# A diffusion step on one core: a third of four weight folds in the opening stage, projection inputs two tiles ahead, attention products two units behind the scores, queries one unit earlier

## The chip, the cores and the metric

The kernel runs on one core of a Trainium2 chip. The metric is the device time of one execution in microseconds (us). The times before are 1214.49, 1209.16 and 1210.06, median 1210.06 us. A profile is one execution recorded by the hardware profiler; the engines in it are PE (TensorE), DVE (VectorE), ACT (ScalarE), POOL (GpSimd) and SP (SyncE, which here only issues transfers).

## The reference

The reference is one inference step of a small hybrid backbone: 256 context tokens and 1024 latent tokens, width 1024, two layers, all in f32.

Layer 0 norms and modulates the tokens (a shift, scale and gate from SiLU(c) through a weight matrix), multiplies them by one combined input projection and splits the result into two mixers, each with 8 query heads, 2 key/value heads of 64, and a SiLU gate path. Mixer A is global attention with norms on queries and keys and rotary positions. Mixer B is attention in a window of ±128 tokens, with a learned sink logit for each head. Context tokens read only context; latent tokens read their latent keys (all, or those of the window), the context keys of this step and 256 cached context keys. The gated outputs of both mixers go through one output projection and are added to the tokens.

Layer 1 replaces attention by a Fourier mixer, and a final norm follows:

```
h  = modulate(rms_norm(x))
u  = h @ w_u                       # 1024 -> 4 groups of 256 channels
z  = Re(FFT2(u))                   # over positions and channels of a group
x += gate * ((z * silu(h @ w_g)) @ w_out)
```

## The kernel before, in words

**Tiles.** The 1280 tokens are ten row tiles of 128: tiles 0 to 7 are latent, 8 and 9 context. Matrix products run on PE as three products of a high and a low half (mm3, line 263), so each input and weight is split first: a cast to the high half on ACT or DVE (L275, L277), then a subtraction for the low half on DVE or POOL (L281).

**Folds.** The Fourier transform over the channels of a group is a matrix product with fixed matrices. It is folded into the weights of layer 1 ahead of their use: for each of the four channel groups, fold_load brings two 128×1024 tiles of the transposed weight (L542, tile w), fold_piece multiplies a quarter of them with the transform's matrix (L557, tile wa, 8 matmuls a piece, four pieces a fold), and fold_put stores the result to DRAM (L547, wd), from which layer 1 reads it. Folds 0 and 1 are done in the opening, folds 2 and 3 during attention.

**The opening stage.** PH0 (L32) is a list of operations written out by hand, in which the program runs them: f, the loads of a fold; F, a piece of a fold; G, a store of two pieces; w and s, the loads of projection weights and the end of their split; x and N, the loads and norms of tokens; L, A and M, the loads, matmuls and end of the modulation (ada, L467; modt, L516; the modulation vectors, L479 and L484); T, the transposes of normed tokens (xt, L424), and X, Y, Z their modulation; K and R, parts of the first projection (kv0s, kv2s, L526); S, small loads. SP issues transfers in the order of the list; the order on the other engines is the scheduler's.

**Order elsewhere.** The framework orders the instructions of each engine with a list scheduler that runs on a timeline of its own, so a small change of the program re-orders every engine. Buffers come from zones (ZONES, L23): a zone holds a number of buffers, and an instruction that takes one waits until its last user is through. The zone q (queries) holds two, the zone p (scores and probabilities) four.

**Attention.** A unit is one row tile, one key/value head and one pair of query heads (t, g, pr); a mixer has 40. `attend` (L1077) runs over a list of units. For each it issues the score matmuls and the softmax (`soft`, L932: sL and sC, L924, and sB, L996, on PE; L958 and L1002 on DVE; the exponential, L965, on ACT), keeps the unit pending, and issues the transposes of the probabilities and the products with the values (`weigh`, L1031: pt, L1041, and av, L1047, on PE; the split of pt on ACT, L275, and DVE, L1044; the result, L1058) once more than LAG units are pending: LAG_A = 1 in mixer A, LAG_B = 3 in mixer B. The queries of a tile and head come from DRAM (load_q, tile q); `attend` loads the next ones when it is at pair QPRE of the present tile:

```python
            if pr == QPRE and nx is not None and nx not in qs and ("q", nx[0] // 2 * 2, nx[1]) in fl_.done:
                qs[nx] = load_q(*nx)
```

**Filler.** After each unit a queue of other work is pumped by a budget of microseconds (FILL_A, FILL_B, FILL_C), so that PE has matmuls while softmax runs on the other engines: gates and queries, then the late folds named in FLATE (L65), then the output projection, tile by tile. An item with a condition (`ready=`) holds up the queue until the condition is met.

**Output projection.** It runs over ten row tiles in five pairs, (0,4), (2,6), (3,7), (1,5), (8,9). proj_load (L1306, through proj_in, L1206) brings a tile's attention result, gate and softmax total (od, gd, scd) from DRAM and scales them on DVE (L1216, L1217), before the split on ACT (L275) and POOL or DVE; proj_step (L1315, through out_proj, L1230) is the projection itself (oz, L263), its results taken out by DVE (L1238, L1239). Each tile's load is queued just ahead of the step of the tile before. can_run (L1379) lets an item run within attention only for the first two pairs, and only when the attention units it reads have been through for some units; what is left is run after attention by `fl_.drain()`.

Of the kernel before, what the change touches and what calls it, by code (L numbers as in the profile page):

```python
# [22 lines left out]
ZONES = {"u": (26, 1032), "w": (8, 1032), "q": (2, 1024), "pt": (3, 1024), "p": (4, 1280), "h": (9, 512), "e": (4, 256)}  # L23
BIG = ("w", "q", "pt", "p", "u")
UV = ("u",)
FILL_A, FILL_B, LAG_A, LAG_B = 4.4, 2.9, 1, 3
E_PH, E_OH, E_OL, E_WO = "a", "a", "dp", "a"
EARLY, SPAN = 1, 2
WSTEP = ((2, 1, 2), (1, 0, 1))
ORD_B = (0, 2, 3, 4, 7, 6, 5, 1, 8, 9)  # L30
AT_K, AT_Q, AT_X, NX1, GL = 1, 2, 5, 7, 3
PH0 = """f0 S0 x0 N0 f1 L0 F00 F01 F02 F03 w0 L1 F10 F11 F12 F13 x1 A0 T0 T1 s0 M0 X0 X1 T2 L2 N1 K0 K1  # L32
 A1 T3 M1 G00 G01 G10 G11 L3 X2 X3 K2 K3 Y0 R0 Y1 R1 w1 S1 T4 A2 x2 N2 Y2 T5 M2 R2 X4 Y3 X5 R3
 K4 Y4 K5 A3 T6 Y5 M3 R4 X6 T7 R5 X7 Y6 K6 Y7 K7 R6 R7"""
S1 = """s1 S2 V Z0 Z1 c0 I0 a2 Z2 Z3 c1 I2 a1 q0 P Z4 Z5 I4 a2 P Z6 Z7 I6 a1 q2 P a2 P k8 a2 P a3 P a9 P"""
ADA_Z = (("p", "pt", "q"),) * 4
# [1 line left out]
XZ = ("u", "u", ("p", "pt", "q"))  # L38
E_ML = ("dp", "dp", "d")
E_MF, E_MH, LC0 = "da", "d", "ppd"  # L40
EF = 2
QPRE, HOLD = 1, 0
PLACE = (
    ((0, 0, 128),), ((128, 0, 128),), ((385, 0, 127), (256, 127, 1)), ((257, 0, 128),), ((769, 1, 127), (512, 0, 1)),
    ((896, 0, 128),), ((641, 0, 128),), ((513, 0, 128),), ((1024, 0, 128),), ((1153, 0, 127), (1152, 127, 1)),
# [16 lines left out]
FILL_C, NLATE = 2.9, 8  # L62
E_FQ, E_GD = "d", "d"
ORDER = "qa0 qa1 kb0 qb0 qb1 g0 g1 g2 g3"
FLATE = "f2 f3"  # L65
AT_B = "s"
AT_F = (0, 1, 2)
AT_N, AT_Z = (0, 0, 3, 0, 3, 2, 2, 2, 2, 2, 3, 3, 3), ("p", "pt", "q")
# [71 lines left out]
def hybrid_step(ctx: ExitStack, tc: tile.TileContext, I, O):  # L140
# [15 lines left out]
    def take(tag, shape, dt=F32):  # L156
        tags = (tag,) if isinstance(tag, str) else tag
        z = min((t for t in tags if spare[t]), key=lambda t: spare[t][0])
        i = spare[z].popleft()[1]
        size = 2 if dt == BF16 else 4  # L160
        for s in shape[1:]:
            size *= s
        assert size <= 4 * ZONES[z][1]
        made[0] += 1
        return Buf(z, i, up.tile(list(shape), dt, tag=f"{z}{i}", name=f"{z}{made[0]}", bufs=1))

    def drop(*bufs):
        for b in bufs:
            stamp[0] += 1
            spare[b.zone].append((stamp[0], b.idx))  # L170
# [380 lines left out]
    def fold_piece(g, kb2, wu, first=False):  # L551
        f = fold["f"]
        acc = bank("t" if first else "g", f"wa{g}{kb2}")
        for i in range(2):
            c0 = (2 * kb2 + i) * P
            for j in range(2):
                pe.matmul(  # L557
                    acc[:, i * 256 : i * 256 + 256], wu[j][:, c0 : c0 + P], f[:, j, :], start=j == 0, stop=j == 1
                )
        if first:  # L560
            if kb2 % 2 == 0:
                early[g, kb2 // 2] = take("u", (P, 4, 256))
            wo = early[g, kb2 // 2][:, 2 * (kb2 % 2) : 2 * (kb2 % 2) + 2, :]
        else:
            wb = take("h", (P, 2, 256))
            wo = wb.a
        copy("wo", "a", wo, acc.rearrange("p (i f) -> p i f", i=2))
        if not first:
            fold_put(g, kb2 * 256, wo)
            drop(wb)  # L570
        if kb2 == 3:
            drop(*wu)
            fold["n"] = fold.get("n", 0) + 1
            if fold["n"] in (EF, 4):
                drop(f)
                del fold["f"]
# [35 lines left out]
    def first_step(op):  # L612
        nm, i = op[0], int(op[1:])
        if nm == "L":
            ada[i] = ada_load(i, ADA_Z[i])
        elif nm == "S":
            small_loads(i)
        elif nm == "x":
            load_x(i, XZ[i])
        elif nm == "N":  # L620
            norm_rows(i)
        elif nm == "w":
            W[i] = load_w(w0cols((C_KA, C_QA)[i]), lc=LC0, later=w_fin.setdefault(i, []))
        elif nm == "s":
            for fin in w_fin[i]:
                fin()
        elif nm == "f":
            wu0[i] = fold_load(i, 2)
        elif nm == "F":
            fold_piece(i // 10, i % 10, wu0[i // 10], True)  # L630
        elif nm == "G":
            e = early.pop((i // 10, i % 10))
            fold_put(i // 10, i % 10 * 512, e.a)
            drop(e)
        elif nm == "A":
            ada_chunk(i, ada.pop(i))
        elif nm == "M":
            ada_fin(i)
        elif nm == "T":
            XT[0, i] = x_T(0, i)  # L640
        elif nm in "XYZ":
            g = "XYZ".index(nm)
            mod_T(g, i, E_ML[g])
        elif nm in "KR":
            t = 4 * "KR".index(nm)
            gemm_chunk(acc0[t], t, W[0], i)
            gemm_chunk(acc0[t + 2], t + 2, W[0], i)
        else:
            return False
        return True  # L650

    region = tc.manual_schedule(engines={sp.engine})
    region.__enter__()
    for op in PH0.split():
        first_step(op)
# [184 lines left out]
    fl_ = Filler()  # L840
# [343 lines left out]
    OB, late = [("u", "w")], [False]  # L1184
# [21 lines left out]
    def proj_in(src, gate, r, resid):  # L1206
        if gate is not None:
            flush_held()
            ol = take(OB[0], (P, 8, P))
            sp.dma_start(ol.a, src[r])  # L1210
            gl = take(OB[0], (P, 8, P))
            rl = take(OB[0], (P, 8, P))
            sp.dma_start(gl.a, gate[r])
            for h in range(2):
                sp.dma_start(rl[64 * h : 64 * h + 64], scd[r, h].partition_broadcast(64))
            pick("pm", XE["pm"]).tensor_mul(gl.a, gl.a, rl.a)  # L1216
            pick("pm", XE["pm"]).tensor_mul(ol.a, ol.a, gl.a)  # L1217
            drop(gl, rl)
        hi, lo = take(OB[0], (P, 8, P), F32R), take(OB[0], (P, 8, P), F32R)
        if gate is not None:  # L1220
            split(hi.a, lo.a, ol.a, E_OH, E_OL)
            drop(ol)
        else:
            for c in range(2):
                split(hi[:, 4 * c : 4 * c + 4, :], lo[:, 4 * c : 4 * c + 4, :], src(c, r), "a", "d")
        xr = take(OB[0], (P, D))
        sp.dma_start(xr.a, resid[r * P : (r + 1) * P, :])
        return hi, lo, xr
# [77 lines left out]
    def proj_load(i, j):  # L1306
        r = pairs[i][j]
        v = r // 8
        if v not in gt0:
            gt0[v] = take(OB[0], (P, D))  # L1310
            sp.dma_start(gt0[v].a, gtd[0, v].partition_broadcast(P))
        ins[r] = proj_in(od, gd, r, I["xp"])
        return 0
# [65 lines left out]
    def can_run(i, j):  # L1379
        r = pairs[i][j]  # L1380

        def fn():
            if sum(len(spare[z]) for z in OB[0]) < NSP or i > EARLY:
                return False
            return all(finished.get(t, 99) + SPAN < clock[0] for t in USES[r])
        return fn

    wgs = []
    steps = [(i, j) for i in range(5) for j in range(2)]

    def late_fold(nm):
        def fn():
            ws[nm] = fold_load(int(nm[1]))
            return 0
        return fn

    for n, nm in enumerate(FLATE.split()):
        fl_.add(0.0, late_fold(nm))
        if n == 0:
            fl_.add(0.0, lambda: proj_load(0, 0), ready=can_run(0, 0))  # L1400
        for k in range(4):
            fl_.add(FC, lambda k=k, nm=nm: fold_piece(int(nm[1]), k, ws[nm]))
    if not FLATE:
        fl_.add(0.0, lambda: proj_load(0, 0), ready=can_run(0, 0))
    for n, ij in enumerate(steps):
        if n == 8:
            fl_.add(0.0, lambda: wgs.append(load_w(I["w_g1"][:, 0:256], tags=BIG)) or 0)
        if n < 9:
            fl_.add(0.0, lambda ij=steps[n + 1]: proj_load(*ij), ready=can_run(*steps[n + 1]))
        fl_.add(7.7, lambda ij=ij: proj_step(*ij))  # L1410

    units = [(t, g, pr) for g in range(2) for t in range(NT) for pr in range(2)]
# [542 lines left out]
```

## Time and profile before

| | |
|---|---|
| times of the runs | 1214.49, 1209.16, 1210.06 us; median 1210.06 |
| the profiled execution: time, span | 1214.27 us, 1212.4 us |
| mean granted clock of PE | 0.985 |
| PE busy | 1166.8 us, 96% |
| DVE, ACT, POOL busy | 839.6, 576.6, 320.1 us |
| DMA traffic | 168.81 MB, mean 139 GB/s |
| mixer B's attention | about 540 to 815 us |

The span is the recorded part of the profiled execution; the rest of its time, 1.9 us, lies around it. A wait is the idle time of an engine ahead of an instruction, put down to the instruction or transfer that released it. The granted clock is the share of full speed at which PE was allowed to run, and a window's value is the mean over it. Sums of busy time count overlapping matmuls once; a group's duration in the timeline includes the end of its last matmul, so the pace of a stream is read from the starts.

### The profile page before, as it was taken

The page shows a single profiled execution, that of the slowest core. Times are in us where ns is not written, and L with a number is a line of the kernel's source. Part 1 is how long each engine was busy: PE and PEld are TensorE (multiplying, and loading weights), DVE is VectorE, ACT ScalarE, POOL GpSimd, SP SyncE. Part 2 cuts the span into 40 slices and gives each one's busy share as a digit, 9 for nine tenths or more (in the row PEclk, how much of TensorE's full clock was granted, in tenths as well). Part 3 has the DMA queues.
Part 4 walks back from the last instruction along what each step waited for, and adds up shares of the span by engine and source line. Part 5 has one row for each costly group of instructions (what it writes and reads, how often), then busy time and mean ns, then how long its engine had stood idle before and what let it go on. Part 6 is the DMA issues. An engine that isn't in the chain of part 4 may idle for free. (4 is left out here: it accounts for less than half of the span.)

```text
span 1212.4 us, 22083 instructions
## 1 busy us (share of the span) xinstructions
PE 1166.8 (96%) x8103; PEld 1041.6 (86%) x8103; DVE 839.6 (69%) x2000; ACT 576.6 (48%) x1159; POOL 320.1 (26%) x278
## 2 busy tenths in 40 slices
PE   7999999999999999999999999989999999999997
PEld 5787899999999998999888887868877888997886
DVE  3479788877777777678787776878756953367543
ACT  3343466555655555556566675533364224342211
POOL 2255634512332130011010114213202217245001
PEclk9899999999999999999999999989999999999999
DMA  9957412323523233344253686677214435264321
GB/s 317 360 190 260 150 59 66 103 79 108 149 64 101 60 92 113 95 120 121 74 140 81 181 256 198 181 201 219 96 44 136 152 114 169 94 200 151 121 103 53
DMA packets 129840, 168.81 MB, mean 139 GB/s; under 512 B 26298, under 2 KB 86454, under 8 KB 129732
## 3 DMA queue, kind: packets, MB, share of 16 engines
q1 hardware_dynamic: 129732, 167.40, 45.5%
q8 instruction: 64, 1.05, 0.4%
q14 instruction: 44, 0.36, 0.1%
HBM read 123.19 MB, written 44.16 MB: 138 GB/s over the span
## 5 line engine op out<-in xcount | busy, mean ns | idle before, releaser
L1044 DVE TENSOR_TENSOR pt<-pt,pt 128x512 fp32r<-128x512 f32 (+1 forms) x264 | 170.8, 658 | 50.9 <-ACT pt L275 50.1
L275 ACT ACTIVATE pt<-pt 128x512 fp32r<-128x512 f32 (+1 forms) x264 | 146.1, 575 | 83.9 <-PE pt L1041 49.0
L1047 PE MATMUL av<-pt,u 128*128 128x256 f32 x1008 | 167.3, 290 | 1.1 <-DVE e L1058 1.0
L1041 PE MATMUL pt<-identr,p 128*128 128x128 f32 x1008 | 153.7, 273 | 1.5 <-DVE pt L1044 1.5
L1047 PEld LDWEIGHTS av<-pt,u 128*128 128x128 f32 x1008 | 140.1, 190 | 6.2 <-DVE e L1058 2.0
L263 PE MATMUL q<-w,u 128*128 128x256 f32 x960 | 143.4, 287 | 0.2 <-ACT h L725 0.2
L263 PEld LDWEIGHTS q<-w,u 128*128 128x128 f32 x960 | 126.0, 189 | 5.1 <-issue 0.8
L1041 PEld LDWEIGHTS pt<-identr,p 128*128 128x128 f32 x1008 | 118.7, 141 | 7.0 <-issue 1.8
L263 PE MATMUL ga<-u,w 128*128 128x512 f32 (+1 forms) x576 | 124.2, 360 | 0.3 <-DVE h L817 0.2
L965 ACT ACTIVATE p<-p,nm 128x1280 f32<-128x1280 f32 (+1 forms) x80 | 95.3, 1192 | 53.4 <-DVE p L958 52.9
L263 PEld LDWEIGHTS ga<-u,w 128*128 128x128 f32 x576 | 93.6, 188 | 15.1 <-ACT pt L275 0.4
L281 POOL TENSOR_TENSOR w<-h,w 128x512 fp32r<-128x512 f32 x38 | 50.1, 1334 | 130.9 <-DVE w L277 100.4
L924 PE MATMUL sL<-u,q 128*128 128x512 f32 x256 | 82.4, 409 | 1.6 <-DMA q<-qd 1.6
L281 POOL TENSOR_TENSOR u<-h,u 128x512 fp32r<-128x512 f32 x24 | 33.8, 1416 | 158.7 <-ACT u L275 151.8
L965 ACT ACTIVATE p<-p,NM 128x640 f32<-128x640 f32 (+2 forms) x80 | 59.1, 739 | 24.5 <-DVE p L958 24.3
L924 PE MATMUL sC<-u,q 128*128 128x256 f32 x320 | 63.4, 297 | 4.0 <-DVE p L1002 2.0
L263 PE MATMUL oz<-u,u 128*128 128x512 f32 x208 | 60.8, 397 | 2.9 <-DVE h L1238 2.9
L263 PE MATMUL oz<-u,w 128*128 128x512 f32 x192 | 58.3, 396 | 0.0
L958 DVE TENSOR_SCALAR_CACHE_REDUCE p<-sL 128x512 f32<-128x512 f32 x64 | 43.8, 685 | 20.1 <-PE sL L924 15.3
L924 PEld LDWEIGHTS sC<-u,q 128*128 128x128 f32 x320 | 49.5, 190 | 7.7 <-DVE p L1002 2.6
L698 POOL TENSOR_TENSOR h<-h,rope 128x512 f32<-128x512 f32 (+1 forms) x18 | 21.2, 1180 | 128.2 <-ACT h L781 82.3
L958 DVE TENSOR_SCALAR_CACHE_REDUCE p<-sL,nm 128x512 f32<-128x512 f32 x64 | 47.6, 744 | 8.3 <-PE sL L924 7.0
(721 smaller groups left out, 2584.3 us busy)
## 6 DMA issues: line engine op xcount, KB each, us to landing
q<-qd SPq DMA_DIRECT2D x80, 256.0 KB
h<-i_w_in SPq DMA_DIRECT2D x40, 256.0 KB
p<-i_ada_w SPq DMA_DIRECT2D x18, 512.0 KB
qd<-q SPq DMA_DIRECT2D x36, 256.0 KB
h<-i_w_out SPq DMA_DIRECT2D x32, 256.0 KB
pt<-i_ada_w SPq DMA_DIRECT2D x15, 512.0 KB
q<-i_ada_w SPq DMA_DIRECT2D x11, 512.0 KB
u<-g1d SPq DMA_DIRECT2D x9, 512.0 KB
```

The lines of the kernel that those rows point to most:

```text
L263: pe.matmul(out, a, b, start=i == 0, stop=i == n - 1)
L275: act.activation(out, in_, AF.Copy)
L281: pick("lo" + lc, lc).tensor_sub(dst_l, src, dst_h)
L698: pick("rope", XE["rope"]).tensor_mul(t1.rearrange("p t h (b c) -> p t (h b) c", b=2), y.rearrange("p t h (b c) -> p t (h b) c", b=2), cb)
L924: pe.matmul(ps, q_at(q, s, hc), keys, start=s == 0, stop=s == 1)
L958: dve.tensor_scalar(p[i][:, end[i] : end[i] + n], ps, sign, last[i], op0=ALU.mult, op1=ALU.min, accum_out=c)
L965: act.activation(p[i][:, 0 : end[i]], p[i][:, 0 : end[i]], AF.Exp, bias=last[i], scale=-1.0, accum_out=SU[:, t, hd + i, 0:1],)
L1041: pe.transpose(tp[:, jj * 256 + i * P : jj * 256 + i * P + P], p[i][:, off : off + P], ident)
L1044: dve.tensor_sub(pt[:, 1, 0:n], tp[:, 0:n], pt[:, 0, 0:n])
L1047: pe.matmul(acc, vv, pt[:, s, jj * 256 : jj * 256 + 256], start=c + jj + s == 0, stop=c + jj == nt - 1 and s == 1,)
```

## The change

Four edits. (1) The third fold moves from the filler of the attention stage to the opening: f2, its loads, stands after the pieces of fold 0 and ahead of w0; F20 to F23, its pieces, stand around M0, X0, X1 and T2; G20 and G21, its stores, stand after R2. EF, the number of folds after which the opening gives back the transform's matrix, goes from 2 to 3, and FLATE loses f2. (2) QPRE goes from 1 to 0, so the next queries are loaded one unit earlier. (3) LAG_B goes from 3 to 2. (4) With AHEAD = 2 a projection tile's input is loaded two tiles ahead of its step instead of one, but only for items that run after attention (late[0] is set there); within attention it stays one ahead.

```diff
-FILL_A, FILL_B, LAG_A, LAG_B = 4.4, 2.9, 1, 3
+FILL_A, FILL_B, LAG_A, LAG_B = 4.4, 2.9, 1, 2
...
-PH0 = """f0 S0 x0 N0 f1 L0 F00 F01 F02 F03 w0 L1 F10 F11 F12 F13 x1 A0 T0 T1 s0 M0 X0 X1 T2 L2 N1 K0 K1
- A1 T3 M1 G00 G01 G10 G11 L3 X2 X3 K2 K3 Y0 R0 Y1 R1 w1 S1 T4 A2 x2 N2 Y2 T5 M2 R2 X4 Y3 X5 R3
+PH0 = """f0 S0 x0 N0 f1 L0 F00 F01 F02 F03 f2 w0 L1 F10 F11 F12 F13 x1 A0 T0 T1 s0 F20 M0 F21 X0 X1 T2 F22 F23 L2 N1 K0 K1
+ A1 T3 M1 G00 G01 G10 G11 L3 X2 X3 K2 K3 Y0 R0 Y1 R1 w1 S1 T4 A2 x2 N2 Y2 T5 M2 R2 G20 G21 X4 Y3 X5 R3
...
-EF = 2
-QPRE, HOLD = 1, 0
+EF = 3
+QPRE, HOLD, AHEAD = 0, 0, 2
...
-FLATE = "f2 f3"
+FLATE = "f3"
...
+    loaded = [0]
+
+    def load_to(n):
+        while loaded[0] <= min(n, 9):
+            proj_load(*steps[loaded[0]])
+            loaded[0] += 1
+        return 0
...
         if n == 0:
-            fl_.add(0.0, lambda: proj_load(0, 0), ready=can_run(0, 0))
+            fl_.add(0.0, lambda: load_to(0), ready=can_run(0, 0))
...
         if n < 9:
-            fl_.add(0.0, lambda ij=steps[n + 1]: proj_load(*ij), ready=can_run(*steps[n + 1]))
+            fl_.add(0.0, lambda n=n: load_to(n + (AHEAD if late[0] else 1)), ready=can_run(*steps[n + 1]))
         fl_.add(7.7, lambda ij=ij: proj_step(*ij))
```

Both programs have the same number of instructions on each engine; what differs is their order and the buffers they use.

More of the change, by code (lines that the diff above doesn't have):

```diff
@@ L1403, in hybrid_step @@
     if not FLATE:
-        fl_.add(0.0, lambda: proj_load(0, 0), ready=can_run(0, 0))
+        fl_.add(0.0, lambda: load_to(0), ready=can_run(0, 0))
     for n, ij in enumerate(steps):
```

## The prediction

> **What bounds the kernel now.** I read the page first, for the bound.
>
> ```profile
> span 1212.4 us, 22083 instructions
> ...
> PE 1166.8 (96%) x8103; PEld 1041.6 (86%) x8103; DVE 839.6 (69%) x2000; ACT 576.6 (48%) x1159; POOL 320.1 (26%) x278
> ```
>
> TensorE is busy in 96% of the span and nothing else is near. So 1212.4 − 1166.8 = 45.6 us are all that waits can give, plus what matmuls lose where the granted clock falls. A change that leaves the matmuls alone can only fill or close holes. The waits of PE say where the holes are (total, times, longest).
>
> ```profile
> PE wa L557 <- DMA w<-i_wuT: 5.9, 2, 4.9
> PE oz L263 <- ACT pt L275: 4.1, 1, 4.1
> ...
> PE sC L924 <- DVE p L1002: 2.0, 1, 2.0
> PE sC L924 <- DMA q<-qd: 2.0, 1, 2.0
> ...
> PE sL L924 <- DMA q<-qd: 1.6, 3, 0.9
> ```
>
> Most are single events of 2 to 4 us. The third view, busy time by window with the granted clock, shows that several cost more than their length, because TensorE runs slower behind them (window, its length, PE busy, ..., clock, DMA share, GB/s).
>
> ```profile
> 22.00:28.00 6.00, 4.13 (x74) 2.71 (x73) 3.94 (x5) 0.88 (x2) 2.65 (x2) 1.00 1.09 347
> 28.00:35.00 7.00, 6.33 (x48) 4.75 (x48) 3.18 (x7) 1.74 (x3) 2.92 (x2) 0.51 1.06 392
> ...
> 42.00:49.00 7.00, 6.51 (x32) 5.83 (x32) 4.67 (x9) 1.51 (x4) 2.37 (x2) 0.52 1.08 378
> 49.00:70.00 21.00, 20.73 (x244) 17.66 (x244) 10.21 (x19) 8.64 (x14) 8.45 (x7) 1.00 1.01 342
> ...
> 619.00:625.00 6.00, 3.33 (x14) 3.04 (x15) 5.35 (x15) 5.67 (x12) 1.21 (x1) 0.76 0.65 184
> ...
> 700.00:708.00 8.00, 8.00 (x57) 7.55 (x56) 5.21 (x18) 5.50 (x16) 0.00 (x0) 1.00 0.70 189
> 708.00:715.00 7.00, 5.04 (x21) 4.30 (x21) 3.70 (x9) 3.25 (x7) 4.70 (x2) 0.76 1.05 336
> ...
> 808.00:820.00 12.00, 7.01 (x18) 5.23 (x19) 10.82 (x22) 5.11 (x8) 2.98 (x2) 0.58 0.58 179
> ```
>
> There are four places: the opening (22 to 49 us), where the clock stands at half twice and the DMA engines are full; 619 us; 708 us; and 808 us, where the projection begins to run without attention beside it. The change touches each of them. I cost it place by place. The sum is made against the profiled execution, 1214.27 us with its span of 1212.4, and set against the median, 1210.06, since it is a difference; the median lies 4.2 below that execution, and a change under 0.5% (6 us) is about what a measurement of this kernel cannot tell from none.
>
> **A. One fold less during attention.** The timeline of PE, in the middle of mixer B's attention:
>
> ```profile
> 702.21 1.89 PE L557 MATMUL wa<-h,w 128*128 128x256 f32 x8
> 703.75 0.47 PE L1047 MATMUL av<-pt,u 128*128 128x256 f32 x1
> ```
>
> One piece of a fold holds PE for 703.75 − 702.21 = 1.54 us. A fold has four pieces: 6.2 us. The stage is bound by PE (8.00 of 8.00 us busy in 700 to 708), so what leaves it shortens it: −6.2. The holes that these pieces filled are priced under F.
>
> **B. The fold in the opening.** There it must fit into holes. Timeline of PE, then of DVE:
>
> ```profile
> 14.98 7.14 PE L557 MATMUL wa<-h,w 128*128 128x256 f32 x32 [0.96 <-DMA w<-i_wuT]
> ...
> 25.81 0.33 PE L516 MATMUL modt<-identr,e 128*128 128x128 f32 x1
> 28.39 1.09 PE L424 MATMUL xt<-identr,u 128*128 128x128 f32 x4 [2.25 <-DVE moda L484]
> ...
> 40.82 0.50 PE L526 MATMUL kv0s<-w,u 128*128 128x256 f32 x2 [1.38 <-ACT u L437]
> ...
> 42.49 1.94 PE L424 MATMUL xt<-identr,u 128*128 128x128 f32 x8 [0.94 <-DVE u L418]
> ```
>
> ```profile
> 24.45 1.65 DVE L277 CAST w<-h 128x512 fp32r<-128x512 f32 x2 [0.33 <-DMA h<-i_w_in]
> 26.14 1.63 DVE L281 TENSOR_TENSOR w<-h,w 128x512 fp32r<-128x512 f32 x1
> 27.69 0.41 DVE L277 CAST w<-h 128x512 fp32r<-128x512 f32 x1
> ...
> 28.10 0.15 DVE L484 TENSOR_TENSOR moda<-modt,bT 128x4 f32<-128x4 f32 x1
> ```
>
> A whole fold (32 matmuls) takes 7.1 us of PE there, 1.8 a piece. The hole at 26 to 28.4 us is there because DVE takes the modulation (L479, L484) behind casts of the first projection weights, and after it PE runs at half clock. TensorE's order at this place in the opening, before, names being tiles (modt the modulation, xt the transposed input, kv0s and kv2s the first projection, ada the modulation's matmuls):
>
> ```order
> L516 MATMUL modt0_329<-identr_85,e40_309 128x128
> L424 MATMUL xt02_344<-identr_85,u6_134 128x128
> L424 MATMUL xt02_344<-identr_85,u7_135 128x128
> L424 MATMUL xt02_344<-identr_85,u8_136 128x128
> L424 MATMUL xt02_344<-identr_85,u9_137 128x128
> L467 MATMUL ada1_407<-pt30_234,e2_114 32x128 x2
> L526 MATMUL kv0s_117<-w22_222,u41_334 128x256
> ```
>
> The same place after, with wa2 the pieces of the moved fold:
>
> ```order
> L557 MATMUL wa20_335<-h3_123,w22_222 128x256
> L557 MATMUL wa20_335<-h3_123,w23_223 128x256
> L516 MATMUL modt0_342<-identr_85,e42_315 128x128
> L557 MATMUL wa21_347<-h3_123,w22_222 128x256
> L557 MATMUL wa21_347<-h3_123,w23_223 128x256
> L557 MATMUL wa21_347<-h3_123,w22_222 128x256
> L557 MATMUL wa21_347<-h3_123,w23_223 128x256
> L526 MATMUL kv0s_117<-w24_228,u44_353 128x256
> ```
>
> The piece wa21 now stands in the hole behind modt, wa20 stands ahead of modt and delays it by its 1.8 us, and wa22 and wa23 follow a few rows later. The holes here add up to 2.25 + 1.38 + 0.94 = 4.6 us, and half clock costs 6.33 × 0.49 = 3.1 in 28 to 35 and 6.51 × 0.48 = 3.1 in 42 to 49: 10.8 together. The ends: none of it recovered, +7.1; all of it, 7.1 − 10.8 = −3.7. Walking the new order by these durations, the hole of 2.25 shrinks to about 0.7 (wa21 fills 1.8 of a chain that DVE still holds), and the first fall of the clock should go: 7.1 − 1.55 − 3.1 = +2.4; without the second fall too, −0.7. I take **+1**. Beyond +7.1: the fold's weights are 2 × 128×1024 floats, 1.05 MB, loaded ahead of w0, and at the 347 GB/s of this window that is 3.0 us by which everything loaded behind comes later; the bad end is +10.1.
>
> Its stores (G20, G21) go to the SP queue behind x2.
>
> ```profile
> 37.44 5.78 SPq L547 DMA_DIRECT2D wd<-u x4
> ```
>
> Four such stores took 5.78 us of SP, so two are 2.9, by which loads queued behind them start later. They stand past 49 us, where PE is busy 20.73 of 21.00; I cost them at nothing, at most 2.9 if the next loads are late already.
>
> The clock needs a second look, since it decides between −0.7 and +2.4. Another wait of PE, in attention:
>
> ```profile
> 752.93 0.73 PE L263 MATMUL oz<-u,u 128*128 128x512 f32 x2 [2.88 <-DVE h L1238]
> ```
>
> The wait of 2.25 us was followed by a clock of 0.51, and 1.38 with 0.94 by 0.52; behind 2.88 two matmuls took 0.73, near full speed (four took 2.08 at 811.97, below). So the length of a wait alone doesn't decide, and I leave the second fall at even odds. The Trainium skill ("TensorE: Matmul & The Clock Gate", Part 1, The HAM clock gate) says that the clock halves after an idle window of about 3.4 us, in windows that run free of the kernel. The trace disagrees in the opening, where 2.25 us sufficed. By that rule the shorter holes that remain would keep full speed, and the sum below would be 1.7 us lower, −15.4 instead of −13.7.
>
> **C. Queries earlier, and f2's late loads gone.**
>
> ```profile
> 710.86 0.77 PE L924 MATMUL sC<-u,q 128*128 128x256 f32 x2 [1.97 <-DMA q<-qd]
> ```
>
> In 708 to 715 PE is idle 7.00 − 5.04 = 1.96 us and loses 7 × 0.24 = 1.7 to the clock, with the DMA share at 1.05: scores wait for queries that queue behind bulk loads. The change issues queries one unit (6.5 us, below) earlier and takes fold loads out of this stage. All of it is 3.6, and the three small waits of sL add 1.6: between 0 and −5.2. I take **−3.5**: the stall is much shorter than the 6.5 us gained, but the queries' second buffer comes free only when the last scores of the tile before have run.
>
> **D. Products two units behind instead of three.** ACT's exponentials, then DVE's waits for p buffers:
>
> ```profile
> L965 ACT ACTIVATE p<-p,NM x42: 712/820/832, 560.5 to 697.6; 128x640 f32<-128x640 f32 x30, 128x512 f32<-128x512 f32 x12
> ```
>
> ```profile
> DVE p L958 <- PE pt L1041: 8.4, 9, 1.7
> ```
>
> Two exponentials a unit: 21 units in 137 us, 6.5 each. There are four p buffers, and with three units in flight the next unit's DVE work waits for the transposes of an old one, nine times. With two one buffer is spare. The stall of 2.0 us in the window at 619 (scores waiting for DVE's L1002 to empty their bank) is of that family: in 619 to 625 PE is idle 2.67 and loses 6 × 0.24 = 1.4 to the clock, 4.1 together. Gone it is −4.1, unchanged 0; DVE, busy 5.35 of those 6 us, is behind in any case, so I take half, **−2**. The other sign is a rival.
>
> **E. Projection inputs two tiles ahead.** PE and DVE at 808 us:
>
> ```profile
> 806.57 0.62 PE L263 MATMUL oz<-u,w 128*128 128x512 f32 x2
> 807.02 0.42 PE L263 MATMUL oz<-u,u 128*128 128x512 f32 x1
> ...
> 811.97 2.08 PE L263 MATMUL oz<-u,pt 128*128 128x512 f32 x4 [4.06 <-ACT pt L275]
> ```
>
> ```profile
> 802.52 1.23 DVE L1216 TENSOR_TENSOR u<-u,u 128x1024 f32<-128x1024 f32 x1 [4.89 <-DMA u<-scd]
> ...
> 808.25 1.22 DVE L1216 TENSOR_TENSOR pt<-pt,p 128x1024 f32<-128x1024 f32 x1
> 809.62 1.21 DVE L1217 TENSOR_TENSOR p<-p,pt 128x1024 f32<-128x1024 f32 x1
> ```
>
> Two matmuls of oz pass in 807.02 − 806.57 = 0.45, 0.23 each. The 18 of 808 to 820 would take 4.1 us at that pace, not 12: 7.9 lost. The cause is on DVE: row 7's input is scaled (808.25, 809.62) only after the results of the tile before were taken out. DVE's order there, before (L1216 and L1217 scale an input, pt1064 that of row 7, u1073 that of row 1; L1238 takes out a result):
>
> ```order
> L1216 TENSOR_TENSOR u1073_10496<-u1073_10496,u1074_10497 128x1024
> L1238 TENSOR_TENSOR h1056_10352<-oz60_10327,u917_9225 128x512
> L1044 TENSOR_TENSOR pt1046_10285<-pt9_310_10280,pt1046_10285 128x512
> L1239 TENSOR_TENSOR u1010_9959<-u1010_9959,h1056_10352 128x512
> L1217 TENSOR_TENSOR p1072_10494<-p1072_10494,u1073_10496 128x1024
> L1058 TENSOR_TENSOR e1041_10242<-av8_31_10228,e1040_10241 64x256
> L1238 TENSOR_TENSOR h1057_10380<-oz61_10355,u917_9225 128x512
> L1239 TENSOR_TENSOR u1010_9959<-u1010_9959,h1057_10380 128x512
> L1216 TENSOR_TENSOR pt1064_10420<-pt1064_10420,p1065_10421 128x1024
> ```
>
> After, where row 7's input is w1054 and w1055 and row 1's u1068:
>
> ```order
> L1216 TENSOR_TENSOR w1055_10327<-w1055_10327,q1056_10328 128x1024
> L1020 COPY byp8_10250<-tot8_10244 128x16
> L281 TENSOR_TENSOR u1052_10320<-u1048_10310,w1051_10319 128x1024
> L1217 TENSOR_TENSOR w1054_10325<-w1054_10325,w1055_10327 128x1024
> L958 TENSOR_SCALAR p1036_10216,NM_106<-sC9_31_10217,nsink_103 128x256
> L1058 TENSOR_TENSOR e1030_10168<-av1_31_10134,e1029_10167 64x256
> L1044 TENSOR_TENSOR pt1033_10203<-pt8_300_10198,pt1033_10203 128x512
> L1238 TENSOR_TENSOR h1060_10365<-oz60_10340,u926_9292 128x512
> L1044 TENSOR_TENSOR pt1037_10233<-pt8_310_10228,pt1037_10233 128x512
> L1014 TENSOR_TENSOR tot9_10296<-NM_106,sink_102 128x8
> L1216 TENSOR_TENSOR u1068_10433<-u1068_10433,u1069_10434 128x1024
> L1239 TENSOR_TENSOR u1007_9935<-u1007_9935,h1060_10365 128x512
> ```
>
> Row 7's input now comes ahead of oz6's results, so its 2.4 us of DVE and the split on ACT are over before PE needs it. Row 1's L1216 stands behind the first of them; if its transfer is late, as the 4.89 us at 802.52 was, DVE stands still, and so do the results behind it, while PE has oz61, oz31 and oz70 queued, some 55 matmuls, 55 × 0.23 = 12.7 us. I take **−5.5**, about two thirds, between 0 and −7.9: what is late next is the transfers, two tiles' of them at once.
>
> **F. Filler.** The four pieces taken from attention were also what PE did while softmax ran. Two units of row 6 and the last four now have no piece or projection step ready, by the conditions in can_run. One stall as at 619 costs 4.1; none 0. I take **+2.5**.
>
> Sum: −6.2 + 1 − 3.5 − 2 − 5.5 + 2.5 = −13.7; 1210.06 − 13.7 = **1196.4 us**.
>
> **Rivals.** (1) *The opening hides nothing*: the fold's load delays w0 and PE waits for it. For it: DMA shares of 1.06 to 1.09 from 22 to 49 us, and 5.9 us of waits for fold weights already. Against it: the hole at 26 us is of DVE's making, not DMA's. Then B is +10.1 instead of +1: −4.6, 1205.5, no difference that can be told. (2) *The projection still stalls*, since inputs of two tiles come at once, or DVE stands at row 1's. For it: the 4.89 us at 802.52. Against: the 12.7 us of matmuls behind. E is 0: −8.2, 1201.9. (3) *Slower*: with two units of distance the products overtake the exponentials in mixer B, and PE, in order, stands before transposes of probabilities that are not there. For it: DVE was busy 5.35 of 6 us at 619, and PE stood there 2.7. Against: two units are 13 us, while a unit's own chain by rows of this view
>
> ```profile
> 642.88 0.47 DVE L958 TENSOR_SCALAR_CACHE_REDUCE p<-sC,nsink 128x256 f32<-128x256 f32 x1
> ...
> 644.45 0.54 DVE L1002 SCALAR_TENSOR_TENSOR p<-sB,maskf 128x384 f32<-128x384 f32 x1
> ...
> 645.92 0.59 DVE L958 TENSOR_SCALAR_CACHE_REDUCE p<-p,nm 128x384 f32<-128x384 f32 x1
> ```
>
> is twice 0.47 + 0.54 + 0.59 and one exponential of 0.82, 4.0 us. Each event costs 4.1. The sum without D is −11.7; it passes +6 from five events in 40 units on, and six give −11.7 + 24.6 = +12.9, 1223.0.
>
> **Chances and range.** Forecast 0.58, (1) 0.17, (2) 0.12, (3) 0.13. With every term at its good end the sum is −6.2 − 3.7 − 5.2 − 4.1 − 7.9 = −27.1, 1183.0, which needs all at once; the range starts at 1186. Upward it takes in (1) and (2) with their spread and stops at 1212, leaving out most of (3). Faster by over 0.5% means under 1204.0, slower above 1216.1. Of the forecast 0.52 is faster and 0.05 the same; of (1) 0.05, 0.08 and 0.04; of (2) 0.08 and 0.04; of (3) 0.02, 0.03 and 0.08: with rounding 0.67, 0.20, 0.13.
>
> **What the profile after would show.** A: 32 matmuls of wa during attention instead of 64. B: the wait for moda under 1 us, and 28 to 35 us at full clock; wrong if w0's casts wait for DMA for longer. C: no wait of sC for q over 1 us. D: no wait of sC for p L1002, and av or pt not waiting for ACT's exponential; wrong if pt waits for p L965 several times. E: no wait of oz for pt L275 over 1 us. F: small waits near the last units of attention. The prediction is wrong as a whole if new holes of PE in attention add up to more than 14 us.

## The result and the profile after

The changed kernel takes 1201.41 us (median of 4 runs, 1200.21 to 1202.38) where the kernel before takes 1209.87: ratio 0.9922, interval 0.9895 to 0.9948, faster by 8.5 us. A second measurement (e9 below) gave 0.9947, 0.9928 to 0.9966. The forecast was 1196.4 in 1186 to 1212, so the sign is right and about half (e9) to two thirds of the size came. Its terms did much worse than their sum.

The profiled execution after took 1201.21 us, its span is 1199.4 with a mean clock of 0.993. Against the first profile of before the span is 13.0 shorter; 4.4 of that is because that execution of before lay above its median. Three milestones divide it. They stand in the timelines of PE by line and tile, first and last start in us: sL, the wide scores of mixer A, and oz, the output projection. Before:

```profile
L924 PE MATMUL sL<-u,q x256: 387/395/505, 126.3 to 506.6; 128*128 128x512 f32 x128
...
L263 PE MATMUL oz<-u,w x192: 387/393/482, 733.2 to 879.7; 128*128 128x512 f32 x192
```

After:

```profile
L924 PE MATMUL sL<-u,q x256: 387/395/505, 127.5 to 504.5; 128*128 128x512 f32 x128
...
L263 PE MATMUL oz<-u,q x32: 388/394/476, 796.2 to 866.8; 128*128 128x512 f32 x32
```

So the opening is 1.2 longer (126.3 to 127.5), mixer A 3.3 shorter (380.3 to 377.0), and mixer B with the projection 10.8 shorter (373.1 to 362.3). The last stage holds the 6.2 us of the fold that left it, so of its waits only 4.6 went. Against a second profile of the kernel before (e1, 369.3) that stage is 7.0 shorter, and only 0.8 is left for waits. These are PE's windows after, at the places the prediction named (clock, DMA share and GB/s last):

```profile
22.00:28.00 6.00, 5.96 (x83) 4.15 (x81) 0.86 (x2) 0.88 (x3) 0.66 (x1) 1.00 1.07 365
28.00:35.00 7.00, 4.54 (x26) 3.73 (x27) 5.15 (x10) 2.63 (x4) 4.71 (x4) 1.00 1.09 360
619.00:625.00 6.00, 5.71 (x36) 5.04 (x36) 6.00 (x20) 5.49 (x12) 1.29 (x1) 1.00 0.88 229
709.00:719.00 10.00, 6.07 (x31) 5.74 (x31) 4.81 (x17) 4.40 (x12) 4.70 (x2) 0.83 0.88 241
806.00:820.00 14.00, 13.07 (x61) 10.45 (x60) 8.86 (x15) 3.14 (x5) 0.31 (x1) 1.00 0.61 171
```

The stalls at 619 and 808 us are gone, and from 22 to 49 us the clock stays at full. (At 108 to 112 us it is 0.66, where the kernel before shows 1.00 in both of its profiles; e2, without the third fold in the opening, shows 0.50 there.) The stall at 709 is not gone: 3.9 us idle and 1.0 (6.07 × 0.17) lost to the clock, more than before. The waits of PE name what stands there now:

```profile
PE sC L924 <- DMA q<-qd: 4.1, 2, 2.6
PE av L1047 <- DVE e L1058: 3.6, 4, 1.0
...
PE wa L557 <- DVE moda L484: 1.8, 1, 1.8
```

Queries still come late (2.6 and 1.5 us), although they are loaded one unit earlier; products wait for DVE to take out the ones before (they share one PSUM bank; 3.6 us here, 1.0 in the profile before); and the hole of the opening now stands in front of a piece of the fold. DVE's timeline, before and after, shows why it moved and didn't close:

```profile
23.70 0.43 DVE L277 CAST w<-h 128x512 fp32r<-128x512 f32 x1 [6.04 <-DMA h<-i_w_in]
```

```profile
26.83 0.43 DVE L277 CAST w<-h 128x512 fp32r<-128x512 f32 x1 [8.72 <-DMA h<-i_w_in]
...
30.50 0.15 DVE L484 TENSOR_TENSOR moda<-modt,bT 128x4 f32<-128x4 f32 x1
```

The first cast of w0 starts 3.1 us later than before, by the 1.05 MB of the fold's weights ahead of it, which the prediction had at 3.0; moda is 2.4 later. In the eight other profiles with this opening the cast starts at 26.07 to 26.66, 2.4 to 3.0 later.

### The profile page after: what moved, and what is told of

Read it like the earlier page. It is cut to its first block, busy times and chain, and to the rows that moved or that the text cites. A ratio compares the mean times of both kernels' runs of the same rounds, so it can differ in the third digit from the quotient of the medians.

```text
span 1199.4 us, 22048 instructions
## 1 busy us (share of the span) xinstructions
PE 1158.9 (97%) x8103; PEld 1034.8 (86%) x8103; DVE 831.2 (69%) x2000; ACT 578.9 (48%) x1159; POOL 317.9 (27%) x278
## 3 DMA queue, kind: packets, MB, share of 16 engines
q8 instruction: 64, 1.05, 0.4%
## 5 line engine op out<-in xcount | busy, mean ns | idle before, releaser
L275 ACT ACTIVATE pt<-pt 128x512 fp32r<-128x512 f32 (+1 forms) x265 | 147.1, 576 | 94.6 <-PE pt L1041 53.0
L924 PE MATMUL sL<-u,q 128*128 128x512 f32 x256 | 82.2, 408 | 0.0
L965 ACT ACTIVATE p<-p,NM 128x640 f32<-128x640 f32 (+2 forms) x80 | 59.2, 741 | 33.4 <-DVE p L958 33.2
L924 PE MATMUL sC<-u,q 128*128 128x256 f32 x320 | 63.1, 297 | 4.7 <-DMA q<-qd 4.1
L281 POOL TENSOR_TENSOR u<-h,u 128x512 fp32r<-128x512 f32 x20 | 27.2, 1362 | 149.6 <-ACT u L275 138.3
L924 PEld LDWEIGHTS sC<-u,q 128*128 128x128 f32 x320 | 48.7, 191 | 8.1 <-issue 4.7
L263 PE MATMUL of<-u,u 128*128 128x512 f32 x150 | 48.6, 395 | 0.4 <-DVE u L1782 0.3
```

What stands on the lines that cost most here:

```text
L263: pe.matmul(out, a, b, start=i == 0, stop=i == n - 1)
L275: act.activation(out, in_, AF.Copy)
L281: pick("lo" + lc, lc).tensor_sub(dst_l, src, dst_h)
L924: pe.matmul(ps, q_at(q, s, hc), keys, start=s == 0, stop=s == 1)
L965: act.activation(p[i][:, 0 : end[i]], p[i][:, 0 : end[i]], AF.Exp, bias=last[i], scale=-1.0, accum_out=SU[:, t, hd + i, 0:1],)
```

## The experiments

All ratios are to the kernel before on the same chip. "Mixer B" in the table is last sL to last oz of each profile. "Lost" is PE's loss from 524 to 880 us: over windows of 4 us, the length less the busy time, plus the busy time times the part of the clock that is missing. It is read from one execution each, as "mixer B" is, so a difference of 1 or 2 us says little; e1 and e9 show how far two executions of one kernel differ.

| kernel | median us | ratio (95%) | mixer B us | lost us |
|---|---|---|---|---|
| before, first profile | 1209.87 | 1 | 373.1 | 21.4 |
| after, first profile | 1201.41 | 0.9922 (0.9895 to 0.9948) | 362.3 | 16.1 |
| e1 before again | 1210.31 | 0.9995 (0.9975 to 1.0014) | 369.3 | 18.2 |
| e2 after, fold late | 1207.35 | 0.9968 (0.9950 to 0.9985) | 365.4 | 14.0 |
| e3 after, inputs one tile ahead | 1203.67 | 0.9937 (0.9915 to 0.9959) | 363.8 | 19.6 |
| e4 after, products three units behind | 1209.76 | 0.9992 (0.9974 to 1.0011) | 371.1 | 25.2 |
| e5 after, queries as before | 1207.78 | 0.9968 (0.9950 to 0.9986) | 365.2 | 19.0 |
| e6 after, no third fold | 1199.44 | 0.9902 (0.9883 to 0.9920) | 365.5 | 20.3 |
| e7 after, three p buffers | 1204.80 | 0.9942 (0.9925 to 0.9959) | 366.9 | 23.5 |
| e8 before, products two units behind | 1201.89 | 0.9921 (0.9907 to 0.9935) | 362.8 | 10.2 |
| e9 after again | 1203.81 | 0.9947 (0.9928 to 0.9966) | 364.8 | 19.6 |
| e10 before, fold in the opening | 1223.97 | 1.0116 (1.0092 to 1.0140) | 380.0 | 33.2 |
| e11 before, lag two and fold | 1210.10 | 1.0000 (0.9982 to 1.0017) | 366.6 | 21.3 |
| e12 after, less filler a unit | 1205.72 | 0.9963 (0.9946 to 0.9981) | 361.4 | 16.1 |

**e1, before again.** No edit.

> The kernel before, unchanged, profiled a second time, because its first profiled execution (1214.27 us) lies 4.4 above the median of its runs (1209.87). Theory: the 4.4 us are a sporadic loss in one place, most likely one of the two stretches of half clock in the opening (3.1 us each, at 28 to 35 and 42 to 49 us); then one of them is at full speed here, the span is near 1208, and the stalls at 619, 708 and 808 us are as they were. Rival: the holes are all the same and the 4.4 us lie spread over the span or outside it; then both stretches show 0.5 again. Ratio to the kernel before: 1.000.

The span is 1208.5. The first stretch of half clock is shorter (0.76 in 28 to 35 us instead of 0.51), the second is there (0.62), and the stalls are each a little smaller: 1.3 instead of 2.0 at 620, 3.4 instead of 4.1 at 808. Both guesses hold in part: the 4.4 us are spread. Prices read from one execution were high by some 3 us in mixer B alone (21.4 lost against 18.2).

**e2, the fold back in attention.**

```diff
-EF = 3
+EF = 2
-FLATE = "f3"
+FLATE = "f2 f3"
```

with PH0 as before.

> The kernel after with the third fold back in attention. Theory: the fold's move is worth 6.2 in attention less 1 to 1.2 in the opening (the first scores come at 127.5 us after, 126.3 before), so this kernel is 5.0 slower than after, 1206.4. Rival (the opening pays nearly all of it, the stage that lost the pieces has holes in their place): 1201 to 1203. Second rival (all the gain is the fold's): 1209.9.

0.9968 against 0.9922 and 0.9947: the move is worth 2.5 to 5.6 us in the company of the other edits; the interval overlaps that of the second ratio, so the lower figure isn't clear of noise. The profiles put 1.9 of it in mixer B on the mean of the two of after (365.4 against 363.6), not 6.2 less a little.

**e3, one tile ahead.**

```diff
-QPRE, HOLD, AHEAD = 0, 0, 2
+QPRE, HOLD, AHEAD = 0, 0, 1
```

> The kernel after with projection inputs one tile ahead everywhere. Theory: the stall of oz for pt L275 near 808 us, 7.9 us with its half clock, comes back, and the small waits of av for e L1058 (3.6) stay: 5 to 8 slower than after, 1206 to 1209. Rival (the stall was closed by the other order that the two-unit lag gives, not by the second tile): 1201 to 1202.

0.9937, between the two ratios of after, so the second tile is worth next to nothing, within the 2 to 3 us of these intervals. The wait of oz for pt L275 doesn't come back; three waits on DVE's L1058 stand at 798 to 804 us instead (1.9, 2.3 and 1.5). The theory falls, the rival holds.

**e4, three units behind.**

```diff
-FILL_A, FILL_B, LAG_A, LAG_B = 4.4, 2.9, 1, 2
+FILL_A, FILL_B, LAG_A, LAG_B = 4.4, 2.9, 1, 3
```

> The kernel after with the products three units behind the scores again. Theory: the stall of sC for p L1002 near 619 us (4.1 with its clock) comes back and the four waits of av for e L1058 (3.6 together) go: 0 to 4 slower than after, 1201.4 to 1205.5. Rival (slower side of the forecast: two units are too few, the new waits of 666, 689 and 729 us and those of av come from it): 2 to 5 faster than after, 1196 to 1199.

0.9992: without this edit nothing is left of the gain. It costs 5.4 to 8.5 us, more than the theory's bound, and the rival, that two units are too few, is refuted. DVE's waits in mixer B show it standing for p buffers that old units still hold, a wait that the kernel after doesn't have:

```profile
DVE p L958 <- PE pt L1041: 5.0, 3, 2.8
```

**e5, queries as before.**

```diff
-QPRE, HOLD, AHEAD = 0, 0, 2
+QPRE, HOLD, AHEAD = 1, 0, 2
```

> The kernel after with the next queries loaded at the second pair of a tile again. Theory: loading them one unit earlier closes no stall, since sC waits for q by 2.6 and 1.5 us near 711 and 717 us in the kernel after too, behind the inputs of the projection's first tiles on the same DMA engines; so the time is that of after within 3, 1198.5 to 1204.5. Rival (the forecast's term C): the stalls grow by 3.5, 1205. Second rival: one unit earlier costs something, because the load waits on SP's queue for its buffer with everything behind it; then 2 to 5 faster than after.

0.9968, 2.5 to 5.6 slower than after (as in e2, the lower figure isn't clear of noise). The rival's size is right, but not its place: sC waits at 720 and 726 us for 2.6 and 2.6 against 2.6 and 1.5, and mixer A (first to last sL) takes 382.3 instead of 377.0. Over thirteen of the fourteen profiles mixer A takes 380.3 to 382.3 with the queries as before (six profiles) and 377.0 to 378.4 with them earlier (seven): 3.3 us on the mean. The fourteenth, e6, has the queries earlier and takes 379.9, but its first sL comes 4 to 9 us sooner than in the others. So the earlier queries seem to pay in mixer A, where sL waited for q only 1.6 us before. PE's idle time and clock loss between the two milestones account for 1.8 of the 3.3 (2.3 on the mean against 0.5); the rest can be work that fell on the other side of a milestone.

**e6, no third fold at all.**

```diff
-            wu0[i] = fold_load(i, 2)
+            if i != 2:
+                wu0[i] = fold_load(i, 2)
...
-            fold_piece(i // 10, i % 10, wu0[i // 10], True)
+            if i // 10 != 2:
+                fold_piece(i // 10, i % 10, wu0[i // 10], True)
```

The lines that adapt the fold's count and its two stores aren't shown.

> The kernel after without the third fold's loads and pieces in the opening; its two stores are issued as before, but store fold 0's results, so the third fold isn't computed at all. It gives the price of the fold in the opening. Theory: 1 to 2.4 faster than after (the forecast's B, and 1.2 by the first scores), 1199 to 1200.5, the hole before moda of 2.2 us and the half clock behind it being back. Rival (the opening pays the fold in full): 7.1 faster, 1194; with its transfer 10.1, 1191.

0.9902, 2.4 us under the first ratio of after and 5.4 under the second. The hole before moda and the half clock behind it are back (0.52 in 28 to 35 us). So the opening does hide part of the fold's 7.1, and B's +1 was somewhat low; the two ratios don't allow a closer price. The milestones show why one is hard to get:

```profile
L927 PE MATMUL sL<-u,q x256: 387/394/504, 121.6 to 501.5; 128*128 128x512 f32 x128
```

(L927 here is L924 elsewhere.) The first sL comes 5.9 and 6.9 us ahead of the two profiles of after, the last one 3.0 and 5.2 ahead. But e2, which has the same two folds in its opening, has its first sL at 127.6 and its last at 505.7, no better than after. Orders of the same work differ by as much as the fold costs.

**e7, three p buffers for two units.**

```diff
+    held_p = take("p", (P, 2, 640))
+    dve.tensor_scalar(held_p[:, 0, 0:8], nsink, 1.0, None, op0=ALU.mult)
     attend([(t, g, pr) for t, g in seq for pr in range(2)], fill, LAG_B, after)
```

The buffer is given back after mixer B's attention.

> The kernel after (products two units behind) with one of the four p buffers held through mixer B's attention, so that three are left for two units, as four were for three. Theory: what a distance of three units cost (8.4 us against after) is the p buffer that the next unit's DVE work waits for until the transposes of the oldest one are done; then DVE p L958 waits for PE pt L1041 again (none in mixer B after, 5.0 us with three units), and the time is 5 to 9 above after, 1206 to 1210. Rival (it is the order of the products themselves, the latency from scores to results): as after, 1200 to 1203.

The wait is back, and larger than in e4:

```profile
DVE p L958 <- PE pt L1041: 6.1, 5, 2.6
```

But the time is 0.9942, within the two ratios of after and clear of e4's. The p buffers aren't what three units cost, or only a small part of it: by the ratios at most the 2.4 us by which this one lies above the lower one of after. My theory of the distance falls.

**e8, two units behind alone.** The diff of e4 in reverse, on the kernel before.

> The kernel before with the products two units behind, nothing else of the change. Theory: taken alone it is worth most of what it is worth in the kernel after, 4 to 8: 1202 to 1207, the stall of sC for p L1002 near 620 us (1.3 to 2.0, with half clock 4) being gone. Rival (it only pays together with the other edits): 1209 to 1212. The forecast's term D: 1208.

0.9921: by itself this edit is as fast as the whole change, and the other three together add nothing to it. Two of them alone on top of it, the earlier queries and the second tile, make e2, which at 0.9968 is 5.7 us slower than e8 with intervals that don't touch. The profile, by the same two rows:

```profile
L924 PE MATMUL sL<-u,q x256: 387/395/505, 126.3 to 506.9; 128*128 128x512 f32 x128
...
L263 PE MATMUL oz<-u,w x192: 387/394/481, 742.1 to 869.7; 128*128 128x512 f32 x192
```

The opening and mixer A are those of before; mixer B is 362.8 instead of 369.3 to 373.1. The stall at 808 us is gone too, though the projection's inputs are loaded one tile ahead. The last products of attention start at 806.59 us, in e1 at 811.98. The largest stall that is left is the queries', near the same place:

```profile
717.30 1.03 PE L924 MATMUL sC<-u,q 128*128 128x256 f32 x4 [5.06 <-DMA q<-qd]
```

**e9, after again.** No edit.

> The kernel after, unchanged, on the chip of the three kernels below, for a narrower ratio and a second profile. Expected ratio 0.992. In the opening the same program left the clock at full in one profile (28 to 35 us, behind a hole of 2.5 us) and at 0.65 to 0.76 in profiles of kernels with the same opening: if that is chance, this profile may show either, and the times spread over 1199 to 1204.

12 runs from 1199.17 to 1208.21. The profile shows one source of this spread. PE's hole in the opening is the same as in the first profile of after, but the clock behind it isn't:

```profile
30.12 3.47 PE L557 MATMUL wa<-h,w 128*128 128x256 f32 x8 [1.81 <-DVE moda L484]
```

```profile
28.00:35.00 7.00, 5.19 (x22) 4.06 (x23) 4.34 (x10) 2.04 (x3) 4.19 (x3) 0.76 1.09 364
```

**e10, the fold in the opening alone.** The diff of e2 in reverse, on the kernel before.

> The kernel before with the third fold moved to the opening, nothing else. Theory (the forecast's A, B and F): -6.2 + 1 to 2.4 + 2.5, 1207.5 to 1209. Rival (taking it out of the kernel after costs 5.6 us, so it is worth as much here): 1204 to 1206. Second rival (the pieces hid waits in an attention whose products are three units behind, which come out now): as before or slower, 1210 to 1214.

1.0116: 14 us slower, past even the second rival. The opening is no worse (first sL at 125.4, full clock from 22 to 49 us), mixer A is as before; the loss lies in mixer B and the projection:

```profile
L924 PE MATMUL sL<-u,q x256: 388/396/503, 125.4 to 506.3; 128*128 128x512 f32 x128
...
L263 PE MATMUL oz<-u,w x208: 387/395/628, 719.7 to 886.3; 128*128 128x512 f32 x104
```

380.0 instead of 369.3, with 6.2 us less work in it. PE's waits from 524 to 880 us have a new first row, five waits where the kernel before had one of 1.0:

```profile
PE av L1047 <- DVE e L1058: 9.0, 5, 4.0
```

The timelines of PE and DVE at the end of attention show what stands behind the two longest of them:

```profile
813.29 1.04 PE L1047 MATMUL av<-pt,u 128*128 128x256 f32 x4 [3.96 <-DVE e L1058]
817.09 1.22 PE L1047 MATMUL av<-pt,u 128*128 128x256 f32 x4 [2.75 <-DVE e L1058]
819.42 0.90 PE L1269 MATMUL eoE<-identr,q 128*128 128x128 f32 x3 [1.11 <-DVE q L1365]
821.64 2.07 PE L263 MATMUL oz<-u,pt 128*128 128x512 f32 x4 [1.32 <-ACT pt L275]
```

```profile
810.42 1.22 DVE L1216 TENSOR_TENSOR u<-u,u 128x1024 f32<-128x1024 f32 x1 [1.93 <-issue]
811.56 1.28 DVE L1044 TENSOR_TENSOR pt<-pt,pt 128x512 fp32r<-128x512 f32 x2
812.76 0.15 DVE L251 SCALAR_TENSOR_TENSOR r11y<-r11w,r11y 128x2 f32<-128x2 f32 x1
812.83 0.41 DVE L1058 TENSOR_TENSOR e<-av,e 64x256 f32<-64x256 f32 x1
813.16 1.21 DVE L1217 TENSOR_TENSOR p<-p,u 128x1024 f32<-128x1024 f32 x1
814.30 1.27 DVE L1352 SCALAR_TENSOR_TENSOR w<-w,r11y,w 128x1024 f32<-128x1024 f32 x1
815.49 1.21 DVE L1216 TENSOR_TENSOR pt<-pt,p 128x1024 f32<-128x1024 f32 x1
816.63 0.41 DVE L1058 TENSOR_TENSOR e<-av,e 64x256 f32<-64x256 f32 x1
```

The last units' products need one PSUM bank in turn. DVE empties it in 0.41 us, but its queue has other work of 1.2 us a piece ahead of that, the scaling of projection inputs (L1216, L1217) and layer 1's norm of finished tiles (L1352): three pieces between 813.16 and 816.63, while PE waits 2.75. In the wait of 3.96 DVE itself stands for 1.93 us ahead of such a piece, for a reason that the profile doesn't show, with the emptying of the bank behind it. These waits grew by 8.0 us against e1, about half of the 14.9 by which the loss grew; the rest is smaller waits and the clock. With the fold's pieces gone the projection starts sooner (the first oz at 719.7 instead of 731.8 in e1), and that more of its DVE work then falls among the last units of attention fits. It isn't shown that the earlier start alone does it: in the kernel after the first oz comes at 720.5 and these waits are 3.6, in e11 at 727.0 and they are 8.0.

**e11, lag and fold.** Both edits on the kernel before.

> The kernel before with the products two units behind and the third fold in the opening, without the earlier queries and without the second tile ahead. If terms add, 9.6 (lag alone) and 5.0 (fold): 1195.5 to 1198. Rival (what the fold gives comes back as waits in attention: idle and half clock from 524 to 880 us lose 10.2 us with the lag alone, 16.1 in the kernel after): 1200 to 1203, with a loss there of 15 us or more.

1.0000. The terms don't add: the lag gives 9.6, and the fold on top takes all of it back. The rival's loss is there (21.3 us lost, av waiting for L1058 8.0), and the time is even above its range. In the one profile the opening is slow too (first sL at 130.0). The kernel after is this one with the earlier queries and the second tile: there the two gain 6.4 to 9.4 us, where they cost 5.7 in e2 against e8.

**e12, less filler a unit.**

```diff
-FILL_A, FILL_B, LAG_A, LAG_B = 4.4, 2.9, 1, 2
+FILL_A, FILL_B, LAG_A, LAG_B = 4.4, 2.75, 1, 2
```

> The kernel after with the filler's budget in mixer B at 2.75 us a unit instead of 2.9, which stretches the filler by the 5.2 us of budget that the fold's four pieces had (32 units by 0.15). Theory (the forecast's F: the filler is used up or blocked too early): the loss from 524 to 880 us falls from 16.1 toward 10, 1196 to 1199. Rival (its waits depend on which instruction comes behind which, not on how much filler there is): 1199 to 1206, the loss as large as before with the waits at other places.

0.9963, not to be told from e9 on the same chip, with 16.1 us lost as in the first profile of after, at other places (3.3 for queries at 716, 2.8 for h L1238 at 842). Stretching the filler by this much (32 × 0.15 is 4.8 us, not 5.2) doesn't lower the loss, though the profiled execution is the fastest of its twelve; the rival holds.

## Why the prediction was right, and where it was not

**A (−6.2) is the step that failed.** "The stage is bound by PE (8.00 of 8.00 us busy in 700 to 708), so what leaves it shortens it". PE was busy where the pieces ran, but the stage doesn't end there. In e10 the largest new waits come 100 us later, where attention's last products and the projection's inputs share DVE. Taking the pieces out lengthened mixer B and the projection by 10.7 us without the shorter lag (e10 against e1, 380.0 and 369.3), lengthened it by 3.8 with it (e11 against e8, 366.6 and 362.8), and shortened it by 1.9 in company of all edits (e2). The pieces did leave; the waits grew by as much or more: PE's loss by 14.9, 11.1 and 3.8 us in these three pairs. Term F (+2.5, bounded at +4.1) was meant to hold this and was too small by several times in the first two.

**B (+1).** Over nine profiles with the moved fold the first sL comes at 125.4 to 130.6, 127.9 on the mean, over four of the late one at 125.8 to 127.6, 126.5: +1.4; e6's times say 2.4 to 5.4. The forecast was close by the first measure and low by the second. Of its parts, the transfer was right (3.0 forecast, 2.4 to 3.1 measured) and the second fall of the clock is gone. The hole wasn't: walked to about 0.7 us, it is 1.8 in the profile after and 0.4 to 2.4 over the nine, since casts of w0 that come later still stand ahead of moda on DVE. The wait for moda under 1 us, the sign that the prediction named, didn't show.

**C (−3.5): size near by luck, place wrong.** Mixer A gave −3.3 between its milestones, of which the prediction had counted 1.6 and the waits explain 1.8. The stall at 709 us that carried the term stayed, against the sign that it named (no wait of sC for q over 1 us), in every kernel with earlier queries (4.1 us of waits in after, 4.4 in e2). In time the edit is worth 2.5 to 5.6 beside the three others (e5) and 7.6 on top of lag and fold (e3 against e11). One unit ahead isn't what it lacks. The clock's part was also reckoned otherwise than in B, on the length of the window and not on PE's busy time: by B's way it is 1.2 in C and not 1.7, and 0.8 in D and not 1.4.

**D (−2): right sign, mis-sized.** The bound was −4.1, the price of one stall. The 8.4 us of waits for p buffers that stood beside it are the whole execution's: 3.3 of them, four waits, lie in mixer B. Alone the edit measured −9.6 (e8), in company −5.4 to −8.5 (e4). Of e1's stalls at 620 (1.3), 692 (1.9), 709 (1.9), 751 (2.0) and 809 us (3.4, and 1.0 behind it) four are closed in e8, while the queries' at 709 grew to 5.1. Rival (3), too short a distance, found nothing: no wait of pt for ACT's exponential stands in the profile after. Why the projection's stalls go with it isn't settled. e7 leaves little to the p buffers. That each result reaches the projection one unit, 6.5 us, sooner fits, but is only argued. The program has a second candidate: the units still pending after the last scores are weighed one after another with no filler between (`while pend:`), three of them with LAG_B = 3 and two with 2. No run separates the two. What is shown is that this edit by itself gives as much as the four together.

**E (−5.5): mis-sized.** Two tiles ahead were worth next to nothing beside the earlier queries (e3), and some 3.9 us without them (e5 against e11, with intervals that just touch). The shorter distance of the products closes the stall at 808 us too: e8 does it without the second tile. With three units no run has the second tile alone; it and the earlier queries together take 15.0 us off there (e4 against e10). What failed is to price the stall as this edit's alone. Rival (2) had the size, E at 0, but for another reason than late transfers.

So the sum came out near by luck, because the errors had both signs: D gave 3 to 8 us more than its term, A with F gave 2 to 14 less, E some 5 less. The range held, but a rival was missing: fewer pieces in the filler bring what is behind them forward, to where it can meet the last units of attention.

## What to carry to other kernels

A stretch that shows PE busy throughout doesn't make the stage shorter by what is taken from it if waits for other engines grow further on: ask what the queue behind will now meet. Where a scheduler orders every engine, edits don't add: the same edit measured from −5.6 to +14.0 us, by its company; try each alone and each left out before crediting it. A stall has to be read from more than one execution, and tied to the edit by a kernel with that edit alone.

## What the runs showed of the hardware

The same hole of PE in the same program (1.82 and 1.81 us) was followed by a clock of 1.00 once and 0.76 once in 28 to 35 us. Over the nine profiles with this opening, holes of 0.41 to 0.54 us were followed by 1.00 (three: e4, e10, e12) and holes of 1.8 to 2.4 us by 1.00 once and by 0.65 to 0.79 five times. So behind a hole of about 2 us the clock can go either way in one program, which is one source of the spread of this opening (first sL at 125.4 to 130.6). The Trainium skill ("TensorE: Matmul & The Clock Gate", Part 1, The HAM clock gate) says that the gate's windows run free of the kernel; that one hole had both outcomes agrees with it. It puts the idling that is needed at about 3.4 us; here 0.69 and 1.81 us with 0.33 of work between them were enough, so the measurement decides against that figure as a safe limit.
